# Where the second tile's state of GLA and HGRN lies: a buffer of its own, or a slot of the gates' tiles

## The chip, the cores and the metric

One core of a Trainium2 chip runs the whole program in a single launch. The metric is the device time of one execution in microseconds (us), lower is better, as the median of several runs.

## The reference, cut to what matters

Two layers of a decoder run for a prompt of 2048 tokens and for a sample of 8 rows of 8 tokens, with the same weights. Each layer projects its input once and feeds four recurrent mixers (retention, HGRN2, GLA, RWKV-7), gates their outputs, projects them back, and then attends to 256 memory tokens. GLA and HGRN are the same recurrence with different gates:

```python
def step(S, inp):                          # one chunk: q, k, v and the log gates g
    b = jnp.cumsum(gi, axis=2)
    o = einsum('bhjm,bhmv->bhjv', scores, vf) + einsum('bhjk,bhkv->bhjv', qf * exp(b), S)
    S_new = exp(b_last)[..., None] * S + einsum('bhmk,bhmv->bhkv', kf * exp(b_last - b), vf)
    return S_new, o
```

The state `S` is carried from chunk to chunk. The kernel takes chunks of 128 tokens, called tiles here.

## The kernel before, in words

**Tiling.** The prompt is cut into 4 blocks of 512 tokens (4 tiles) per layer, so there are 8 blocks. Block 0 of each layer, called a *sample block* here, also carries the 64 sample tokens. Weights stream through three-slot buffers (`wraw` for the loaded weight, `whl` for its two rounded parts; GpSimd makes the second part, line 227), and the large projections, called *dense* here, go through the two PSUM buffers `psd`.

**Order within a sample block** (`block`, then `gates`, then `finish`). Dense projections for RWKV; RWKV of the prompt in two halves (pool `wk1`), then RWKV of the sample (pool `wk1s`); dense for GLA; GLA of the prompt in two halves of two tiles each (pool `wk2`, opened anew for each half), then GLA of the sample (`wk5`); dense for HGRN (`hg_f`, `hg_q`, `hg_i`); HGRN of the prompt in two halves (`wk3`); dense for retention; retention of all four tiles (`wk4`, `R_ret`); then the gates, which need tiles `oh` of pool `wkf`. In the other blocks GLA and HGRN take all four tiles at once, and pools `wk1s` and `wk5` do not occur there.

**The order of the instructions** is made by a planner at build time. It takes program order as priority, shifted by the table `PRI`, and lets independent chains run beside each other; each engine then executes its own queue strictly in the order planned.

**GLA and HGRN of a half** (`R_gla`, `R_hgrn`): `dyadic` multiplies the gates into the queries and keys level by level and builds the scores `sT` (lines 755 and 838 to 840 in the trace); `totok` turns the keys; `outputs` makes the states `Sx` (memset at line 609, written at line 622), reads them with the queries, and normalizes. `Sx` holds the state of the half's second tile. It comes from pool `wk2` or `wk3` in sample blocks, and from the weight buffers in the others.

**The tag `th`** of the long-lived pool `dnp` has two slots of 2 KB per partition. In program order a sample block asks it for: GLA's keys `dn_gk` (line 1287), four tiles for the sigmoid of `hg_q` (`silu2`, line 523: prompt and sample for each of two column groups), eight tiles `th` of the gates (line 1282), two of the cross-attention. A tile takes whichever slot is free, and the tiles of one tag get their slots in the order in which the program asks.

**Pools on one partition.** Pools on the left side are stacked upward, pools on the right side downward from byte 229,344. By the shapes of their tiles, `wk1s` covers bytes 173,760 to 216,064 and `wk5` 173,760 to 192,576. On the right `wk2` of a sample block takes 12,032 bytes (217,312 to the top), and `wk3` takes 13,312 (216,032 to the top), of which `Sx` has 512 and 1,024. A pool may lie on bytes of one that was closed before it in program order; it then waits until that other pool's tiles there have been used for the last time. `wk4` and `wkf` lie on the bytes of `wk1s` and `wk5`.

Of the kernel before, what the change touches and what calls it, by code (L numbers as in the profile page):

```python
# [10 lines left out]
F32 = mybir.dt.float32  # L11
# [11 lines left out]
TB = 512  # L23
# [110 lines left out]
def decoder(ctx, tc, I, C, O):  # L134
# [7 lines left out]
    def pool(name, bufs=1, **kw):  # L142
        return tc.tile_pool(name=name, bufs=bufs, **kw)
# [42 lines left out]
    dnp = ctx.enter_context(pool("dnp"))  # L186
# [8 lines left out]
    def PS(kind="r"):  # L195
        kind = "d" if kind == "d" else lane[0]
        if kind == "ac":
            kind = "ac"[turn[0]]
            turn[0] ^= 1
        p = {"d": psd, "a": psa, "b": psb, "c": psc}[kind]  # L200
        return p.tile([128, 512], F32, name="ps" + kind, tag=kind)
# [17 lines left out]
    def mm(out, lhsT, rhs, start=True, stop=True):  # L219
        with held():  # L220
            PE.matmul(out, lhsT=lhsT, rhs=rhs, start=start, stop=stop, skip_group_check=True)  # L221
# [4 lines left out]
    def tt(e, out, a, b, op):  # L226
        e.tensor_tensor(out, a, b, op)  # L227
# [16 lines left out]
    for name, (o, shape) in C["layout"].items():  # L244
        n = math.prod(shape[1:])
        x = (u8 if name in U8PACK else ct)[:shape[0], o:o + n]
        if len(shape) > 2:
            ax = "abc"[:len(shape) - 1]
            x = x.rearrange(f"p ({' '.join(ax)}) -> p {' '.join(ax)}", **{k: v for k, v in zip(ax, shape[1:])})
# [35 lines left out]
    def sample_const(name, wp):  # L285
        t = wp.tile(list(C[name].shape), F32, name="s_" + name, tag="s_" + name)
        dma(t, C[name])
        return t
# [252 lines left out]
    def head_norm(o, P, nt, eps, center, wp, sqtag, evac):  # L541
        n4 = nt * NH
        o4 = o.rearrange("p t (h d) -> p (t h) d", d=64)
        st = wp.tile([128, 16], F32, name="hst", tag="hst", bufs=2)
        if center:
            V.tensor_reduce(st[:P, :n4], o4, AX.X, ALU.add)
            V.tensor_scalar(st[:P, :n4], st[:P, :n4], -1.0 / 64, None, ALU.mult)
            tt(V, o4, o4, bc(st[:P, :n4].unsqueeze(2), [P, n4, 64]), ALU.add)
        sq = wp.tile([128, n4, 64], F32, name="hsq", tag=sqtag[0], bufs=sqtag[1])
        A.activation(sq[:P, :n4], o4, AF.Square)  # L550
        ss = wp.tile([128, 16], F32, name="hss", tag="hss", bufs=2)
        V.tensor_reduce(ss[:P, :n4], sq[:P, :n4], AX.X, ALU.add)  # L552
        ri = wp.tile([128, 16], F32, name="hri", tag="hri", bufs=2)
        rsq(ri[:P, :n4], ss[:P, :n4], 1.0 / 64, eps, wp)
        tt(V, o4, o4, bc(ri[:P, :n4].unsqueeze(2), [P, n4, 64]), ALU.mult)
        ps = PS("t").rearrange("p (c n) -> p c n", c=2)
        for c in range(2):
            for t in range(nt):
                tr(ps[:, c, t * P:(t + 1) * P], o[:, t, c * 128:(c + 1) * 128], P)
        evac(ps[:, :, :nt * P])  # L560
# [23 lines left out]
    def masked_q(q, bm, wp):  # L584

        qx = wp.tile([128, SB, SN], F32, name="qx", tag="qx", bufs=2)
        tt(V, qx, bc(q.unsqueeze(1), [128, SB, SN]), bm, ALU.mult)
        return qx

    def expand(v, wp, name):  # L590

        vx = wp.tile([128, SB, 64], F32, name=name, tag=name, bufs=2)
        tt(G, vx[:SN], bc(v.unsqueeze(1), [SN, SB, 64]), bc(K["bmaskT"].unsqueeze(2), [SN, SB, 64]), ALU.mult)
        return vx[:SN].rearrange("p b d -> p (b d)")

    def outputs(seg, score, v, qd, S, NG, NC, kT, tot, wp, eps, center, evac, state_out=None):

        P, nt = seg.P, seg.nt  # L600
        KD = 128 // NG
        NP = NG // 2
        if not seg.sample:
            es = [slice(0, 64), slice(64, 128)]
            if nt > 2 and not center:
                x = wrp.tile([128, nt - 1, NC, 128], F32, name="Sx", tag="w")
            else:
                x = wp.tile([128, nt - 1, NC, 128], F32, name="Sx", tag="Sx")
            G.memset(x, 0.0)
            St = [S] + [x[:, t] for t in range(nt - 1)] + [S]  # L610
            pu = PS("r")[:, :nt * NC * 64].rearrange("p (t c n) -> p t c n", t=nt, c=NC)
            for t in range(nt):
                for h in range(NH):
                    c, g = divmod(h, NG)
                    mm(pu[g * KD:(g + 1) * KD, t, c, :], kT[:, t, h * KD:(h + 1) * KD], v[:, t, h * 64:(h + 1) * 64])

            def move(t):
                for c in range(NC):
                    for p in range(2):
                        gs = slice(64 * p, 64 * p + 64)  # L620
                        a, b = (y[gs, c, p * 64:(p + 1) * 64] for y in St[t:t + 2])
                        V.scalar_tensor_tensor(b, a, tot(t, c)[gs], pu[gs, t, c, :], ALU.mult, ALU.add)  # L622
            for t in range(nt - 1):
                move(t)
            pos = []
            for t0 in range(0, nt, 2):
                po = PS("r").rearrange("p (t n) -> p t n", t=2)
                p5 = po.rearrange("p t (c g j d) -> p t c g j d", c=NC, g=2, j=NP)
                for t in range(t0, t0 + 2):
                    for c in range(NC):  # L630
                        for j in range(NP):
                            for e in es:
                                mm(p5[e, t - t0, c, :, j, :], qd[:, c, j, t * 128 + e.start:t * 128 + e.stop], St[t][:, c, :], True, False)
                            for g in range(2):
                                h = c * NG + g * NP + j
                                x = score(t, h)
                                for e in es:
                                    mm(po[e, t - t0, h * 64:(h + 1) * 64], x[:, e], v[:, t, h * 64:(h + 1) * 64], False, True)
                pos.append(po)
            move(nt - 1)  # L640
            tags = ("rqT", "rkT", None) if center else ("qx2", "qx2", 2)
            for t0, po in zip(range(0, nt, 2), pos):
                o = wp.tile([128, 2, 256], F32, name="osb", tag=tags[0], bufs=tags[2])
                A.activation(o, po, AF.Copy)
                head_norm(o, 128, 2, eps, center, wp, tags[1:], lambda ps: evac(ps, t0 * 128))
            return
        bm = sample_const("bmask", wp)
        pa = PS("r")
        for h in range(NH):
            c, g = divmod(h, NG)  # L650
            mm(pa[:SN, h * 64:(h + 1) * 64], score(0, h), v[:SN, 0, h * 64:(h + 1) * 64])
        o = wp.tile([128, 1, 256], F32, name="osb", tag="osb")
        A.activation(o[:SN, 0], pa[:SN, :256], AF.Copy)
        pg = [PS("r") for _ in range(NG)]
        qx = [masked_q(qd[:, c, :], bm, wp) for c in range(NC)]
        for two in range(0, NH, 2):
            heads = [(j, *divmod((j * NG + two // 2) if NC == 2 else two + j, NG)) for j in range(2)]
            for b in range(SB):
                for j, c, g in heads:
                    gs = slice(g * KD, (g + 1) * KD)  # L660
                    mm(pg[g][j * SN:(j + 1) * SN, :64], qx[c][gs, b, :], S[gs, c, b, :], b == 0, b == SB - 1)
            for j, c, g in heads:
                x = o[:SN, 0, (c * NG + g) * 64:(c * NG + g + 1) * 64]
                tt(V, x, x, pg[g][j * SN:(j + 1) * SN, :64], ALU.add)
        head_norm(o[:SN, 0:1], SN, 1, eps, center, wp, ("hsq", None), evac)
        for c in range(NC):
            pu = PS("r")
            for g in range(NG):
                h = c * NG + g
                vx = expand(v[:SN, 0, h * 64:(h + 1) * 64], wp, "vx")  # L670
                mm(pu[g * KD:(g + 1) * KD, :], kT[:SN, 0, h * KD:(h + 1) * KD], vx)
            tot(c)
            tt(V, S[:, c], S[:, c], pu.rearrange("p (b d) -> p b d", b=SB), ALU.add)
        state_out()
# [1371 lines left out]
```

## Time and profile before

| | us |
|---|---|
| median of 3 runs | 3620.43 |
| lowest, highest | 3615.89, 3628.23 |
| the profiled execution | 3610.52 |
| its span, first to last instruction | 3608.7 |

The granted TensorE clock is 0.956 of full speed over the span. The trace is read by stage: the span is far longer than any wait in it, and the change touches only two stretches, the sample blocks of layer 0 (about 140 to 500 us of the span) and of layer 1 (about 1880 to 2260 us). PE stands for TensorE's matmuls, DVE for VectorE, ACT for ScalarE, POOL for GpSimd.

### The profile page before, as it was taken

What the parts mean: (1) busy time and instruction counts of PE and PEld (TensorE: products, weight loads), DVE (VectorE), ACT (ScalarE), POOL (GpSimd) and SP (SyncE); (2) the same over time, 40 slices, a digit from 0 to 9 for tenths busy, and PEclk for the clock granted to TensorE, in tenths of its full rate; (3) what the DMA queues carried; (4) which work ended last, traced back from release to release, by engine and by line L of the source; (5) the groups of instructions that cost most, each with busy time, mean ns of one, the idle gap of its engine ahead of it and who ended that gap; (6) DMA issues with size and microseconds to landing.
All of it is one profiled execution on the core that took longest, in us unless ns stands there. A gap on an engine that the chain in (4) does not pass through costs nothing.

```text
span 3608.7 us, 85093 instructions
## 1 busy us (share of the span) xinstructions
PE 3342.4 (93%) x36126; PEld 2834.0 (79%) x36126; DVE 2069.8 (57%) x5631; ACT 1254.4 (35%) x2655; POOL 538.4 (15%) x632
## 2 busy tenths in 40 slices
PE   7898899999999999999999987999979999999998
PEld 5777687777978888888877856878868788877887
DVE  5665654775436744575456456467653467446754
ACT  4442234322243324332344323443322433244323
POOL 3313230111000100011122232211100011000100
PEclk8999799999999999999999977999989999999999
DMA  6424464236552254325543352542545522543255
GB/s 191 169 88 143 119 228 173 86 90 216 194 196 98 82 193 152 124 73 198 173 172 110 119 156 99 207 145 97 146 150 205 170 98 99 192 148 115 81 201 188
DMA packets 241952, 530.74 MB, mean 147 GB/s; under 512 B 66854, under 2 KB 179750, under 8 KB 197542
## 3 DMA queue, kind: packets, MB, share of 16 engines
q1 hardware_dynamic: 241574, 525.31, 42.6%
q8 instruction: 285, 4.67, 0.5%
q14 instruction: 93, 0.76, 0.1%
HBM read 410.10 MB, written 115.16 MB: 146 GB/s over the span
## 4 chain that ended last, share of the span: by engine, by line
PE 71%; DVE 17%; ACT 5%; issue 4%; DMA 3%; POOL 2%; SPq 0%; ACTq 0%; POOLq 0%; DVEq 0%
PE psd L221 38%; PE psa L221 12%; PE psc L221 11%; PE psb L221 4%; PE psa L263 2%; PE psb L263 2%; PE psc L263 2%; DVE rsq L227 1%; DMA wraw<-in_w_in 1%; DVE Sx L622 1%; POOL whl L227 1%; DVE hss L552 1%; DVE sT L755 1%; DVE osb L227 1%; DVE wosb L227 1%
## 5 line engine op out<-in xcount | busy, mean ns | idle before, releaser
L221 PE MATMUL psd<-act,whl 128*128 128x512 f32 (+1 forms) x4032 | 1014.0, 405 | 29.1 <-DVE th L1283 11.9
L221 PEld LDWEIGHTS psd<-act,whl 128*128 128x128 f32 (+1 forms) x4032 | 751.6, 191 | 211.4 <-issue 22.2
L221 PE MATMUL psd<-whl,act 128*128 128x256 f32 x3840 | 537.7, 293 | 12.3 <-POOL whl L227 8.1
L221 PEld LDWEIGHTS psd<-whl,act 128*128 128x128 f32 x3840 | 487.3, 195 | 38.2 <-issue 16.4
L227 POOL TENSOR_TENSOR whl<-wraw,whl 128x1024 fp32r<-128x1024 f32 (+1 forms) x90 | 216.0, 2406 | 354.3 <-ACT whl L349 343.9
L271 POOL TENSOR_TENSOR ri<-ri,mhalf 128x1 f32<-128x1 f32 (+1 forms) x87 | 49.8, 573 | 1129.0 <-DVE ri L270 1116.1
L221 PE MATMUL psd<-whl,oh 128*128 128x256 f32 x1152 | 211.4, 284 | 0.0
L221 PEld LDWEIGHTS psd<-whl,oh 128*128 128x128 f32 x1152 | 177.7, 189 | 1.1 <-issue 0.3
L221 PE MATMUL psd<-whl,ol 128*128 128x256 f32 x576 | 162.7, 283 | 0.0
L349 ACT ACTIVATE whl<-wraw 128x1024 fp32r<-128x1024 f32 (+1 forms) x90 | 94.2, 1048 | 104.5 <-PE psc L221 35.5
L949 ACT ACTIVATE Xb<-X 32x256 f32<-32x256 f32 (+1 forms) x164 | 67.6, 412 | 143.1 <-DVE X L968 101.8
L221 PE MATMUL psb<-dn_hq,dn_hf 64*64 64x32 f32 (+1 forms) x3840 | 86.4, 234 | 30.9 <-DVE dn_hq L227 9.7
L221 PEld LDWEIGHTS psb<-dn_hq,dn_hf 64*64 64x64 f32 x3840 | 76.1, 149 | 46.8 <-issue 37.8
L221 PEld LDWEIGHTS psd<-whl,ol 128*128 128x128 f32 x576 | 108.6, 189 | 0.0
L227 DVE TENSOR_TENSOR x<-x,psd 128x256 f32<-128x256 f32 x72 | 30.3, 421 | 129.4 <-PE psd L221 129.4
L227 POOL TENSOR_TENSOR tot<-tot 128x8 f32<-128x8 f32 (+7 forms) x128 | 37.4, 293 | 409.1 <-DVE dn_gq L227 179.3
L426 ACT ACTIVATE xs<-xn 128x1024 f32<-128x1024 f32 (+1 forms) x34 | 35.9, 1055 | 173.4 <-PE psb L263 143.8
L755 DVE COPY_PREDICATED sT<-upack,psb 128x256 f32<-128x256 uint8 (+1 forms) x200 | 76.7, 428 | 30.6 <-PE psb L221 29.2
L1283 DVE SCALAR_TENSOR_TENSOR th<-th,psd 128x512 f32<-128x512 f32 x48 | 32.3, 686 | 95.1 <-ACT th L1282 95.0
L221 PEld LDWEIGHTS psd<-hts,wraw 128*64 128x64 f32 x1984 | 67.8, 141 | 20.3 <-issue 9.1
L221 PE MATMUL psa<-whl,oh 128*128 128x256 f32 x448 | 82.8, 283 | 0.0
L221 PE MATMUL psc<-whl,oh 128*128 128x256 f32 x448 | 82.7, 282 | 0.0
(776 smaller groups left out, 6844.7 us busy)
## 6 DMA issues: line engine op xcount, KB each, us to landing
whl<-w_w_out SPq DMA_DIRECT2D x56, 1024.0 KB
wraw<-in_w_in SPq DMA_DIRECT2D x76, 512.0 KB
wraw<-in_w_out SPq DMA_DIRECT2D x32, 512.0 KB
w_w_out<-whl SPq DMA_DIRECT2D x16, 1024.0 KB
x<-x SPq DMA_DIRECT2D x32, 512.0 KB
whl<-w_rw_r SPq DMA_DIRECT2D x12, 1024.0 KB
whl<-w_rw_k SPq DMA_DIRECT2D x12, 1024.0 KB
whl<-w_rw_v SPq DMA_DIRECT2D x12, 1024.0 KB
```

The source lines that it names most:

```text
L221: PE.matmul(out, lhsT=lhsT, rhs=rhs, start=start, stop=stop, skip_group_check=True)
L227: e.tensor_tensor(out, a, b, op)
L263: PE.transpose(out, in_, ident[:rows, :rows])
L271: G.tensor_tensor(y, y, mhalf[:P], ALU.pow)
L349: A.activation(hl[:, 0], raw, AF.Copy)
L426: A.activation(out, xt, AF.Square, accum_out=ss[:P])
L552: V.tensor_reduce(ss[:P, :n4], sq[:P, :n4], AX.X, ALU.add)
L622: V.scalar_tensor_tensor(b, a, tot(t, c)[gs], pu[gs, t, c, :], ALU.mult, ALU.add)
L755: V.copy_predicated(out, bc(mk, [P, w, 32 // s, s]), ps)
L949: A.activation(dst(b), src(b), AF.Copy)
L1283: V.scalar_tensor_tensor(th, th, 1.0, x, ALU.add, ALU.mult)
```

## The change

In `outputs`, for GLA and HGRN in blocks where a part has two tiles, `Sx` is no longer allocated from the part's pool; it is the first 128 or 256 columns of a tile of tag `th` in `dnp`. Retention (`center`) keeps the pool's buffer, and the four-tile blocks keep the weight buffers. `wk2` becomes 512 bytes smaller in sample blocks and `wk3` 1,024 bytes smaller. No instruction is added or removed.

```diff
             if nt > 2 and not center:
                 x = wrp.tile([128, nt - 1, NC, 128], F32, name="Sx", tag="w")
+            elif center:
+                x = wp.tile([128, nt - 1, NC, 128], F32, name="Sx", tag="Sx")
             else:
-                x = wp.tile([128, nt - 1, NC, 128], F32, name="Sx", tag="Sx")
+                x = dnp.tile([128, TB], F32, name="Sx", tag="th", bufs=2)[:, :NC * 128].rearrange("p (t c n) -> p t c n", t=1, c=NC)
             G.memset(x, 0.0)
```

## Rows read from the trace of the kernel before

**Rows 1.** The page's busy time: engine, us, share, instructions; PEld is weight loads.

```profile
PE 3342.4 (93%) x36126; PEld 2834.0 (79%) x36126; DVE 2069.8 (57%) x5631; ACT 1254.4 (35%) x2655; POOL 538.4 (15%) x632
```

**Rows 2.** Busy time by stretch: stretch, us, busy (count) per engine, PE clock, DMA.

```profile
260.00:280.00 20.00, 19.24 (x338) 17.06 (x336) 8.41 (x31) 6.89 (x14) 0.00 (x0) 1.00 0.18 54
...
440.00:460.00 20.00, 11.75 (x238) 10.29 (x240) 15.15 (x57) 3.90 (x10) 2.23 (x7) 0.50 0.01 2
...
2200.00:2220.00 20.00, 11.17 (x216) 9.64 (x216) 15.47 (x56) 6.17 (x14) 1.96 (x7) 0.58 0.01 2
```

**Rows 3.** By tile: HGRN's last input and first step, layer 0 block 0.

```profile
L524 DVE SCALAR_TENSOR_TENSOR dn_hq<-th,psd x2: 679/684/689, 229.5 to 243.1; 128x512 f32<-128x512 f32 x2
...
L838 DVE TENSOR_SCALAR ha<-dn_hf,c,c x4: 395/411/1127, 369.5 to 433.0; 128x256 f32<-128x256 f32 x4
```

**Rows 4.** The same for layer 1 block 0, then layer 0 block 2.

```profile
L524 DVE SCALAR_TENSOR_TENSOR dn_hq<-th,psd x2: 677/682/687, 1961.3 to 1974.9; 128x512 f32<-128x512 f32 x2
...
L838 DVE TENSOR_SCALAR ha<-dn_hf,c,c x4: 398/404/413, 2134.7 to 2190.4; 128x256 f32<-128x256 f32 x4
...
L524 DVE SCALAR_TENSOR_TENSOR dn_hq<-th,psd x2: 674/678/681, 1156.6 to 1168.8; 128x512 f32<-128x512 f32 x2
...
L838 DVE TENSOR_SCALAR ha<-dn_hf,c,c x2: 540/816/1093, 1173.0 to 1181.8; 128x512 f32<-128x512 f32 x2
```

**Rows 5.** Order of time: the end of sample RWKV, then HGRN, in both layers.

```profile
358.26 0.46 POOL L227 TENSOR_TENSOR ons_rwkv<-ons_rwkv,og 128x128 f32<-128x128 f32 x1 [0.31 <-ACT og L1273]
358.66 0.32 POOL L609 MEMSET Sx<- 128x256 f32 x1
...
2134.14 0.42 DVE L227 TENSOR_TENSOR wosb<-wosb,hri 64x256 f32<-64x256 f32 x1
...
2134.68 0.72 DVE L838 TENSOR_SCALAR ha<-dn_hf,c,c 128x256 f32<-128x256 f32 x2
```

**Rows 6.** By tile: retention's first transposes and the gates' first rounding, three blocks.

```profile
L263 PE MATMUL psc<-fpack,dn_rq x8: 272/273/330, 403.0 to 403.9; 128*128 128x128 f32 x8
...
L1486 ACT ACTIVATE oh<-th x8: 614/631/634, 461.7 to 491.4; 128x512 fp32r<-128x512 f32 x8
...
L263 PE MATMUL psc<-fpack,dn_rq x8: 421/421/473, 2164.3 to 2165.8; 128*128 128x128 f32 x8
...
L1486 ACT ACTIVATE oh<-th x8: 612/626/634, 2218.7 to 2250.0; 128x512 fp32r<-128x512 f32 x8
...
L263 PE MATMUL psc<-fpack,dn_rq x8: 272/272/273, 838.1 to 838.9; 128*128 128x128 f32 x8
...
L1486 ACT ACTIVATE oh<-th x8: 617/627/636, 874.4 to 914.8; 128x512 fp32r<-128x512 f32 x8
```

**Rows 7.** HGRN's matmuls in block 1 of layer 0: busy by stretch, two tiles.

```profile
715.00:800.00 85.00, 12.75 (x512) 9.99 (x512) 6.72 (x9) 0.92 0.31 92
...
715.00:800.00 85.00, 4.36 (x96) 3.97 (x96) 1.19 (x2) 0.92 0.31 92
```

**Rows 8.** Order of time: last read of `dn_gk`. By tile: retention's last input.

```profile
252.57 0.38 PE L263 MATMUL psb<-fpack,dn_gk 128*128 128x128 f32 x2
...
L1287 ACT ACTIVATE dn_rv<-psd x2: 597/597/597, 341.4 to 355.7; 128x512 f32<-128x512 f32 x2
```

**Rows 9.** Dense work alone (tile `psd`) in the stretch after `hg_q`'s first sigmoid.

```profile
234.00:254.00 20.00, 13.35 (x103) 10.95 (x103) 1.11 (x3) 1.02 (x3) 1.00 0.38 132
```

**Rows 10.** Order of time: one GLA multiply alone, one beside a GpSimd split.

```profile
235.23 0.38 DVE L227 TENSOR_TENSOR dn_gq<-dn_gq,tot 128x256 f32<-128x256 f32 x1
...
238.83 2.39 POOL L227 TENSOR_TENSOR whl<-wraw,whl 128x1024 fp32r<-128x1024 f32 x1 [2.83 <-ACT whl L349]
...
239.50 2.00 DVE L227 TENSOR_TENSOR dn_gq<-dn_gq,tot 128x256 f32<-128x256 f32 x1
```

**Rows 11.** The gates' first tiles, and half of a dense group of 24 matmuls.

```profile
L1282 ACT ACTIVATE th<-gs x2: 631/632/632, 367.2 to 379.0; 128x512 f32<-128x512 f32 x2
...
405.16 3.02 PE L221 MATMUL psd<-act,whl 128*128 128x512 f32 x12
```

## The prediction, made before the changed kernel was run

> **What bounds the kernel now.** The page first: TensorE has matmuls running for 3342 of 3609 us [rows 1], so time can only come from stretches in which it waits or runs at the lower clock. The table of busy time by stretch shows where these lie: in the middle of a sample block TensorE is busy for 19.24 of 20 us at full clock, but before the gates for 11.75 of 20 us at granted clock 0.50, and in layer 1 for 11.17 at 0.58 [rows 2]. 0.50 is the 1.2 GHz level; before it the engine had only the small matmuls of two recurrences, since the dense work had run out. What runs there? The view by tile answers: HGRN. In layer 0 its last input is ready at 243 us, its first step starts at 369.5 us [rows 3]. In layer 1 it waits from 1975 to 2134.7 us; in an ordinary block from 1168.8 only to 1173.0 us [rows 4].
>
> What does it wait for? The order of time shows that HGRN's memset follows sample RWKV's last GpSimd instruction within 0.4 us, and that in layer 1 `ha` starts 0.5 us after sample RWKV's last use of `hri` [rows 5]. These are bytes: `wk1s` ends at 216,064 and `wk3` begins at 216,032, so 32 bytes of `ha` lie on the last buffer of `hri`. HGRN does not wait for sample GLA (`wk5`), which ends far lower: `ha` starts at 369.5 us, retention, which does lie on `wk5`'s bytes, at 403.0 us [rows 3, 6]. So the wait goes by overlap, not by program order.
>
> **The change part by part.** *Pool `wk3`* loses 1,024 bytes and then begins at 217,056, above `wk1s`. The wait is gone, and HGRN can start when GLA's second half and `hg_q` are done, at about 262 us in layer 0 and 1990 us in layer 1 (estimates: 9 us after `dn_gk`'s last read at 252.6 us [rows 8], since `hg_q` must follow it, see below). It then runs beside the rest of prompt RWKV and beside sample RWKV. `wk2` loses 512 bytes; it overlapped no left pool before, so nothing follows.
>
> What is late next? The chain of the left pools: sample RWKV, sample GLA, retention, then `oh`, each lying on the one before. HGRN's start does not shorten the first two by anything I can read, so I take nothing there. Retention is shortened. Its stage, from first transposes to the first rounding of a gate, takes 461.7 - 403.0 = 58.7 us in layer 0 and 2218.7 - 2164.3 = 54.4 us in layer 1, with HGRN's second half in the same VectorE and TensorE queues; in block 1 of layer 0, where HGRN is over by then, it takes 874.4 - 838.1 = 36.3 us [rows 6]. Gains: 22.4 and 18.1 us, 40.5 us in all.
>
> *The cost of HGRN's new place.* Its matmuls are 12.75 + 4.36 = 17.1 us of TensorE in a block where they run at nearly full clock [rows 7], and they now stand in a stretch where TensorE has 0.8 us in 20 free [rows 2]. All of it would be lost if each matmul pushed the chain of the left pools; nothing, if it pushed only dense work, which has time: retention's last input is ready at 355.7 us and retention starts at 403.0 us, 47 us later [rows 6, 8]. A block therefore pays 0 to 17.1 us. I take 5, near the lower end, because the planner ranks RWKV before HGRN and the dense work has that cover; 10 us for both blocks.
>
> *The two slots of `th`.* Now GLA's `Sx` tiles stand in the line for them. The first gets the free slot after `dn_gk`, long before it is needed. The second takes the slot that the first gives back. Then both slots are held, by `dn_gk` and by `Sx`, and the first sigmoid of `hg_q`, whose product stands at 229.5 us today, must wait for `dn_gk`'s last read at 252.6 us [rows 3, 8]. Behind it the two `psd` buffers fill, and all dense work stops. In that stretch it took 13.35 us of TensorE [rows 9]. What hides this: GLA and RWKV go on alone and faster, and the dense work comes later. With HGRN's share retention's last input moves from 355.7 to about 355.7 + 13.4 + 17.1 = 386 us, still ahead of 403.0 us. I cost it at nothing; if that cover is gone it costs 13.35 us per block. The chain that waits for `dn_gk`'s release, GLA itself, is not held up by anything of the dense work, so no circle forms.
>
> HGRN's two `Sx` tiles take both slots next and give them back at the end of each half, before which no gate can be evaluated. RWKV's two gate tiles used the slots at 367.2 and 379.0 us [rows 11]. HGRN's first half takes 433.0 - 369.5 = 63.5 us today [rows 3]; two such halves from 262 us on end by 389 us (an estimate). The gate tiles may then come up to 22 us late, which is hidden, since `oh` waits for retention's end in any case. Nothing is lost. The memsets stay on GpSimd; HGRN's takes 0.32 us [rows 5], and behind a waiting one stand the weight splits of 2.4 us [rows 10], which the dense work waits for. That wait exists today as well, for a buffer of the pool.
>
> A rule speaks against the new place. A GLA multiply takes 0.38 us alone and 2.00 us when it starts during a GpSimd split [rows 10]. The Trainium skill, "SBUF — State Buffer", section "Who interferes with whom", says that VectorE instructions with two SBUF inputs and GpSimd instructions that read SBUF exclude each other for a whole instruction; these rows agree. HGRN would meet more splits in the dense stage; each costs it 1.6 us, on a chain that is then off the end.
>
> **Sum.** 40.5 - 10 = 30.5 us. The profiled execution took 3610.5 us, 9.9 us below the median, and would take 3580; on the median, 3620.4 - 30.5 = 3590 us. Bounds: with no contention, and with sample GLA in layer 0 (358.7 to 403.0 us, 44 us) as short as in layer 1 (2134.6 to 2164.3 us, 30 us [rows 5, 6]), 40.5 + 14 = 55 us, and some 5 us more if HGRN fills idle TensorE instead of pushing anything: 3560. With the full 17.1 us in each block, 40.5 - 34.2 = 6 us: 3614.
>
> **The rivals.** *No gain, because the slots turn into the new wait.* The dense stop of 13.35 us per block comes back as time: 3620.4 - 30.5 + 26.7 = 3617 us. For it: all dense work goes through two `psd` buffers and one sigmoid blocks them. Against it: the 47 us of cover. It decides when retention's last input is later than the end of sample GLA. The Trainium skill, "Perfetto Trace Analysis", section "Optimization Strategy", says that a gap repeating on the engine that should be saturated can mean that there is not enough SBUF for the next tile; by it, more users of two slots means such gaps.
>
> *Slower: HGRN stays late and holds the slots.* If the 32 bytes are not what HGRN waits for, the change doesn't do what it is read to do. Then HGRN's `Sx` tiles hold both slots from about 262 us until its halves end at about 433.0 us [rows 3] and 461.7 us [rows 6], RWKV's gate tiles at 367.2 and 379.0 us [rows 11] must wait, and the two dense groups of GLA's gates, which lie ready in `psd` today, are made only after that: 2 groups of 2 x 3.02 us [rows 11] in each of two blocks, 24 us: 3645 us. It decides as soon as HGRN's first half ends after 367.2 us. For it: only two blocks show the overlap. Against it: the 0.5 us in layer 1 and the ordinary block.
>
> **How the numbers follow.** The forecast of 3590 us (3560 to 3614) has 0.70, the slots as the new wait 0.18, HGRN late 0.12. The predicted time is 3590 us. The range has to reach the second case, 3617 us, with the measurement's 0.2% above it: 3560 to 3625; it leaves out the third case and some of the ends. A measurement can tell 0.3%, about 11 us, from no change. Faster by more than that 0.70, within it 0.18, slower 0.12.
>
> **What would show it.** Right: `ha` starts near 262 and 1990 us; TensorE is no longer at 0.50 with HGRN's matmuls before the gates; retention's stage falls to about 36 us; `hg_q`'s sigmoids start at about the last read of `dn_gk`; retention's last input is ready before its first transposes. Wrong: `ha` still follows the last `hri` of sample RWKV; RWKV's gate tiles come after HGRN's end; or sample RWKV is longer by more than retention is shorter.

## The result and the profile after

| | before | after |
|---|---|---|
| median | 3618.16 us (4 runs) | 3567.20 us (4 runs) |
| ratio, with its 95% interval | | 0.9868 (0.9848 to 0.9889) |
| the profiled execution, its span | 3610.52, 3608.7 | 3566.24, 3564.4 |
| granted clock over the span | 0.956 | 0.968 |

By the ratio the changed kernel is faster by 1.3%: 48 us, between 40 and 55; the two medians are 51 us apart. The prediction had 3590 us, a gain of 30.5 us, with a range from 3560 to 3625 us. The sign was right, and the overlap as a cause; the size was not, and what made up the difference was not in the sum.

The view by tile of the changed kernel, layer 0 block 0, answers to [rows 3, 6, 8] (line numbers have moved by two):

```profile
L524 DVE SCALAR_TENSOR_TENSOR dn_hq<-th,psd x2: 687/687/687, 251.2 to 260.6; 128x512 f32<-128x512 f32 x2
L840 DVE TENSOR_SCALAR ha<-dn_hf,c,c x4: 410/410/415, 261.8 to 323.3; 128x256 f32<-128x256 f32 x4
L263 PE MATMUL psc<-fpack,dn_rq x8: 421/421/478, 397.3 to 398.9; 128*128 128x128 f32 x8
L1289 ACT ACTIVATE dn_rv<-psd x2: 598/598/599, 404.0 to 409.7; 128x512 f32<-128x512 f32 x2
L1488 ACT ACTIVATE oh<-th x8: 613/633/635, 440.2 to 478.0; 128x512 fp32r<-128x512 f32 x8
```

HGRN's first step stands at 261.8 us, where it stood at 369.5 [rows 3]; the sigmoids of `hg_q` now come after GLA's last use of `dn_gk`. The same for layer 1 block 0, with the copy of `dn_gk` that begins GLA there:

```profile
L1289 ACT ACTIVATE dn_gk<-psd x1: 597/597/597, 1866.1 to 1866.1; 128x512 f32<-128x512 f32 x1
L840 DVE TENSOR_SCALAR ha<-dn_hf,c,c x4: 406/408/410, 1978.9 to 2035.9; 128x256 f32<-128x256 f32 x4
L263 PE MATMUL psc<-fpack,dn_rq x8: 272/273/328, 2138.3 to 2139.2; 128*128 128x128 f32 x8
L1488 ACT ACTIVATE oh<-th x8: 613/631/634, 2171.5 to 2206.6; 128x512 fp32r<-128x512 f32 x8
```

In the kernel before, that copy of `dn_gk` starts here:

```profile
L1287 ACT ACTIVATE dn_gk<-psd x1: 597/597/597, 1883.1 to 1883.1; 128x512 f32<-128x512 f32 x1
```

It splits the 44.3 us between the two spans (3608.7 - 3564.4): 1883.1 - 1866.1 = 17.0 us were gained before it, most of it in layer 0's sample block, and 27.3 us behind it, nearly all of it in layer 1's sample block. By stage, with [rows 6]:

| | layer 0 | layer 1 |
|---|---|---|
| retention starts sooner | 403.0 - 397.3 = 5.7 | 26.0 - 17.0 = 9.0 |
| its stage is shorter | 58.7 - 42.9 = 15.8 | 54.4 - 33.2 = 21.2 |
| gates, first to last rounding, are longer | 29.7 - 37.8 = -8.1 | 31.3 - 35.1 = -3.8 |
| the rest | 3.6 | 0.9 |
| sum | 17.0 | 27.3 |

The busy time by stretch answers to [rows 2] (columns as there); two more stretches are added.

```profile
260.00:280.00 20.00, 19.59 (x440) 17.24 (x438) 14.11 (x42) 7.94 (x17) 4.34 (x7) 1.00 0.23 81
420.00:440.00 20.00, 19.92 (x131) 16.71 (x132) 17.41 (x40) 7.88 (x12) 6.14 (x3) 1.00 0.92 277
440.00:460.00 20.00, 15.72 (x67) 12.61 (x66) 15.55 (x26) 8.28 (x13) 6.05 (x3) 0.91 0.75 270
2160.00:2180.00 20.00, 3.97 (x18) 2.80 (x15) 13.73 (x41) 6.93 (x12) 0.00 (x0) 0.58 0.22 70
2200.00:2220.00 20.00, 19.99 (x154) 19.06 (x153) 11.45 (x17) 6.25 (x11) 9.65 (x4) 1.00 0.84 281
```

The reader is to see two new limits. In layer 0 TensorE is now full before the gates (19.92 of 20 us, at full clock), 17.35 us of it dense work. In layer 1 it has run out of work instead: 3.97 of 20 us at clock 0.58, while retention's last normalizations run mainly on VectorE (13.73 us).

And the dense work in the stretch of [rows 9], where it had 13.35 us:

```profile
234.00:254.00 20.00, 1.66 (x35) 0.66 0.23 81
```

The dense stop that the prediction described is real: 1.66 us of dense work are left there, and the clock fell to 0.66. Nevertheless the kernel is faster than the sum said.

### The profile page after: what moved, and what is told of

Its sections match the earlier page's. It is cut to its first block, busy times and chain, and to the rows that moved or that the text cites. A ratio compares the mean times of both kernels' runs of the same rounds, so it can differ in the third digit from the quotient of the medians.

```text
span 3564.4 us, 85069 instructions
## 1 busy us (share of the span) xinstructions
PE 3314.5 (93%) x36126; PEld 2814.3 (79%) x36126; DVE 2075.4 (58%) x5631; ACT 1253.4 (35%) x2655; POOL 535.9 (15%) x632
## 4 chain that ended last, share of the span: by engine, by line
PE 70%; DVE 18%; ACT 4%; DMA 3%; issue 3%; POOL 2%; SPq 0%; ACTq 0%; POOLq 0%; DVEq 0%
PE psd L221 38%; PE psa L221 11%; PE psc L221 11%; PE psb L221 4%; PE psa L263 2%; PE psb L263 2%; PE psc L263 2%; DVE rsq L227 1%; DVE Sx L624 1%; DMA wraw<-in_w_in 1%; DVE osb L227 1%; DVE hss L552 1%; POOL whl L227 1%; DVE hri L283 1%; DVE sT L757 1%
## 5 line engine op out<-in xcount | busy, mean ns | idle before, releaser
L227 POOL TENSOR_TENSOR tot<-tot 128x16 f32<-128x16 f32 (+7 forms) x128 | 36.4, 284 | 399.3 <-DVE dn_gq L227 182.8
L221 PE MATMUL psb<-dn_hq,dn_hf 64*64 64x32 f32 (+1 forms) x3840 | 78.6, 222 | 6.2 <-DVE dn_hq L227 3.8
L221 PEld LDWEIGHTS psb<-dn_hq,dn_hf 64*64 64x64 f32 x3840 | 68.6, 136 | 19.9 <-issue 11.5
L221 PE MATMUL psd<-hts,wraw 128*64 128x64 f32 x1984 | 79.0, 231 | 3.9 <-DVE th L1285 3.8
```

## The experiments

Four questions: does the overlap by bytes hold HGRN? What does its removal bring alone? What do the slots do, and whose? By what?

### The overlap taken away, without the slots

The kernel before, with the spare buffer of `hri` gone where it has the sample's 64 rows, so that `wk1s` ends at 216,000:

```diff
-        ri = wp.tile([128, 16], F32, name="hri", tag="hri", bufs=2)
+        ri = wp.tile([128, 16], F32, name="hri", tag="hri", bufs=1 if P < 128 else 2)
```

> The kernel before, with one buffer instead of two for `hri` where it has 64 rows (the sample). `Sx` stays in its own buffer; `wk1s` ends at 216,000, below `wk3`'s 216,032. Overlap alone (the slots cost and bring nothing): `ha` of layer 0 starts at about 250 us, since `hg_q` needs no wait for a slot, and the time is that of the changed kernel, 3567 us within 11. Slots as cost: the dense stop behind `dn_gk` is gone, up to 2 x 13 us better than the changed kernel, 3541 us. Slots as help: the gates' tiles come early again and their dense groups stand in front of sample RWKV, which in layer 1 stays some 50 us long instead of 39; 3585 to 3600 us. Something else than the overlap holds HGRN: `ha` at 369 us and 3618 us.

Measured: 3593.05 us, ratio 0.9938 (0.9920 to 0.9956). HGRN's places, by tile, layer 0:

```profile
L524 DVE SCALAR_TENSOR_TENSOR dn_hq<-th,psd x2: 681/684/687, 227.3 to 240.7; 128x512 f32<-128x512 f32 x2
L838 DVE TENSOR_SCALAR ha<-dn_hf,c,c x4: 401/411/1057, 263.5 to 330.5; 128x256 f32<-128x256 f32 x4
```

The overlap did hold HGRN, and freeing it brings 22 us (16 to 29). That is less than the forecast of 30.5 and about half of what the change gains. Of the expectations, slots as help fits in its time, between 3585 and 3600 us, and in sample RWKV of layer 1, which takes even 56.3 us. The reason given for it does not fit: RWKV's gate tiles do not come early (421.8 us in layer 0, 431.6 in the changed kernel, 367.2 before). `ha` came at 263.5 us and not at 250, no sooner than in the changed kernel, though `hg_q` was ready 20 us earlier.

### The same from the other side: 64 bytes

The changed kernel with an unused buffer in `wk3` where HGRN has two tiles, of 1,024 bytes as here or of 960 (`[128, 240]`):

```diff
+                if NC == 2:
+                    wp.tile([128, 256], F32, name="pad", tag="pad")
```

> The changed kernel, with an unused buffer of 1,024 bytes in `wk3` where HGRN has two tiles, so that `wk3` begins at 216,032 as before and overlaps `wk1s`; both `Sx` in the slots. If the overlap holds HGRN: `ha` after the last `hri` of sample RWKV (about 360 us in layer 0), and the slots are held late: the third case of the prediction, 3645 us; at least 3618. If what frees HGRN is that `Sx` left its pool: `ha` at 262 us and 3567 us.

> The changed kernel, with an unused buffer of 960 bytes in `wk3`, 64 bytes less than in the padded kernel that took 3629 us: `wk3` begins at 216,096, above `wk1s`' end at 216,064. If the overlap by bytes decides: `ha` at 262 us and 3567 us. If the size of the pool or its use of memory as such matters: between 3567 and 3629 us.

Measured: 3629.07 us with 1,024 bytes, ratio 1.0034 (1.0021 to 1.0047), and 3568.66 us with 960 bytes, ratio 0.9892 (0.9874 to 0.9910). Layer 0 with 1,024 bytes (line numbers have moved by four):

```profile
L842 DVE TENSOR_SCALAR ha<-dn_hf,c,c x4: 399/400/402, 353.2 to 431.2; 128x256 f32<-128x256 f32 x4
L1286 ACT ACTIVATE th<-gs x2: 629/630/630, 417.1 to 466.0; 128x512 f32<-128x512 f32 x2
```

and with 960 bytes:

```profile
L842 DVE TENSOR_SCALAR ha<-dn_hf,c,c x4: 406/410/415, 257.1 to 317.6; 128x256 f32<-128x256 f32 x4
```

64 bytes of a buffer that nothing reads or writes are worth over 50 us: the ratios differ by 0.0142, 51 us, and the medians by 60 us, of which 4.5 us is the difference between the kernel before in the two rounds of runs (3616.04 and 3611.53 us). The 1,024-byte kernel is the prediction's second rival made real: HGRN late, the gates' tiles (367.2 and 379.0 us in [rows 11]) behind it at 417.1 and 466.0. It is slower than the kernel before by 12 us (8 to 17); the prediction had priced it at 24.

### Whose slots

GLA's `Sx` (`NC == 1`) back in its own pool, HGRN's in the slots; then the other way round (`NC == 2`), with the spare `hri` buffer gone as above, so that `wk3` keeps clear of `wk1s`:

```diff
-            elif center:
+            elif center or NC == 1:
                 x = wp.tile([128, nt - 1, NC, 128], F32, name="Sx", tag="Sx")
```

> The changed kernel, with GLA's `Sx` back in a buffer of pool `wk2`; HGRN's `Sx` stays in a slot of `th`, `wk3` stays above `wk1s`. If GLA's part of the slots costs the dense stop: `hg_q`'s sigmoids at 229 us again and up to 26 us better than the changed kernel, 3541 us. If GLA's slots cost nothing: 3567 us. If the slots of GLA bring something by holding dense work back from RWKV: as the kernel with own buffers and no overlap, above 3580 us.

> The changed kernel, with HGRN's `Sx` back in a buffer of pool `wk3`, GLA's `Sx` in the slots, and one buffer of `hri` for the sample, so that `wk3` at 216,032 lies above `wk1s` (216,000). If HGRN's use of the slots costs or brings nothing: 3567 us within 11. If HGRN's slots, held until its halves end, hold the gates' tiles back (367 us before, 432 us in the changed kernel) and this costs time: RWKV's gate tiles come at about 370 us and the time is 10 to 20 us lower. If this holding back is what shortened sample RWKV: 15 us higher.

Without overlap in any of the four, the medians are:

| | HGRN's `Sx` in its own buffer | in a slot |
|---|---|---|
| GLA's `Sx` in its own buffer | 3593.05 | 3599.13, ratio 0.9953 (0.9939 to 0.9968) |
| in a slot | 3572.03, ratio 0.9884 (0.9864 to 0.9904) | 3567.20 |

HGRN's slots bring and cost nothing that stands out in both rows (+6 and -5 us). GLA's bring 21 to 32 us, so the third expectation of the first kernel (above 3580 us) and the first of the second (3567 within 11) held. The prediction had costed both at nothing, and only feared a loss.

### The wait of `hg_q` taken away, the slots kept

GLA's slots do one thing to others: the sigmoids of `hg_q` have to wait for `dn_gk`'s last read. In this kernel they take the buffer of tag `gs`, in sample blocks only; both `Sx` stay in the slots. In a second kernel, which has `bool(smp) and l == 0` for `bool(smp)`, this is so in layer 0 alone.

```diff
-    def silu2(ps, out, n, wp):
-        th = wp.tile([128, TB], F32, name="th", tag="th", bufs=2)
+    def silu2(ps, out, n, wp, gs=False):
+        th = wp.tile([128, TB], F32, name="th", **(dict(tag="gs") if gs else dict(tag="th", bufs=2)))
...
-                proj_c("hg_q", i * 128, lambda ps: silu2(ps, hq[:, i, :], TB, gp), lambda ps: silu2(ps, hqs[:, i, :], SN, gp))
+                proj_c("hg_q", i * 128, lambda ps: silu2(ps, hq[:, i, :], TB, gp, bool(smp)), lambda ps: silu2(ps, hqs[:, i, :], SN, gp, bool(smp)))
```

> The changed kernel, but in sample blocks the sigmoids of `hg_q` take the buffer of tag `gs` instead of a slot of `th`. Both `Sx` stay in the slots; only the wait of `hg_q` for `dn_gk`'s last read is gone, and with it the dense stop. If that wait is what shortens sample RWKV in layer 1 (by leaving dense work to stand beside it): `hg_q`'s first sigmoid at about 228 us, sample RWKV of layer 1 some 56 us long at a granted clock near 0.8, and the time of the kernel with own buffers and no overlap, 3593 us within 11. If the wait costs time, as the prediction's second case has it: below 3567 us, down to 3541. If the gain comes from something else in the slots: 3567 us.

> As the run before, but only in layer 0; in layer 1 `hg_q` still waits for `dn_gk` in the line for the slots. If the wait brings its gain in layer 1 alone and costs some 3 us in layer 0 (19.7 against 17.0 us gained there): layer 1's sample RWKV is 41 us long at a clock near 1.0 and the time is 3564 us, between 3556 and 3572. If the gain hangs on layer 0's order too: above 3580 us.

> The changed kernel unchanged, on the chip of these runs, as what the three others are compared with: 3567 us within 6.

Measured: 3595.57 us, ratio 0.9956 (0.9943 to 0.9969), without the wait; 3574.24 us, ratio 0.9899 (0.9882 to 0.9916), without it in layer 0 alone; 3565.50 us, ratio 0.9878 (0.9861 to 0.9894), for the changed kernel again. The wait is the cause: taking it away in both layers gives back 30 us, as the first expectation has it, though every `Sx` lies where it lay. Most of it is layer 1's: 21 us lie between the two kernels that differ there alone (3595.57 and 3574.24). Without the wait in layer 0 alone the loss is 9 us, and the time is 2 us above the range that was expected, though layer 1's sample RWKV is as forecast (41.8 us at clock 1.00). The intervals of that kernel and the changed one overlap, and the profiles of the kernels without the wait in layer 0 reach layer 1's `dn_gk` from 2.7 us sooner to 12.6 us later than the changed kernel; so whether the wait gains in layer 0 stays open.

Where does layer 1 lose it? The largest part in sample RWKV. Busy time and clock from its first `vx` to its last GpSimd instruction, first without the wait, in this kernel:

```profile
2073.30:2129.50 56.20, 49.40 (x493) 36.68 (x494) 31.42 (x82) 18.12 (x42) 21.06 (x18) 0.79 0.43 132
```

in the kernel with own buffers and no overlap:

```profile
2060.30:2116.60 56.30, 49.49 (x493) 36.78 (x493) 31.39 (x82) 18.19 (x42) 21.01 (x18) 0.79 0.44 135
```

in the changed kernel:

```profile
2061.10:2102.60 41.50, 38.72 (x536) 29.80 (x529) 31.02 (x95) 15.36 (x39) 17.70 (x19) 1.00 0.42 131
```

and in the kernel before, where HGRN is not yet there:

```profile
2083.20:2136.00 52.80, 47.23 (x326) 29.93 (x326) 28.78 (x64) 16.19 (x33) 24.88 (x16) 0.79 0.60 193
```

With the wait the stretch takes 41.5 us at clock 1.00 (41.4 to 41.8 us in the five profiles with it in layer 1 and no overlap); without it 56.2 to 57.2 us at 0.73 to 0.79 (three profiles). TensorE's work is nearly the same: 49.40 x 0.79 = 39.0 us at full clock, an estimate, against 38.72. So of the 14.7 us, about 49.40 - 38.72 = 10.7 us is the lower clock.

Is it that more dense work stands beside sample RWKV? The same two stretches for dense work alone (TensorE's busy time with its count, clock, DMA), without the wait and in the changed kernel:

```profile
2073.30:2129.50 56.20, 21.35 (x163) 0.79 0.43 132
2061.10:2102.60 41.50, 17.08 (x166) 1.00 0.42 131
```

It is not: there are 163 and 166 dense matmuls, and 21.35 x 0.79 = 16.9 us of work against 17.08. What the wait holds back comes later still. Layer 1 by stage, in us, with the granted clock and the count of dense matmuls:

| | without the wait | changed kernel |
|---|---|---|
| from the copy of `dn_gk` to sample RWKV | 197.5, 0.96, 909 | 195.0, 0.96, 808 |
| sample RWKV | 56.2, 0.79, 163 | 41.5, 1.00, 166 |
| from there to retention's first transposes (sample GLA) | 43.2, 0.83, 83 | 35.7, 0.90, 156 |
| retention's stage | 27.9, 0.62, 0 | 33.2, 0.78, 24 |
| gates, first to last rounding | 34.9, 0.83, 115 | 35.1, 0.82, 115 |
| sum | 359.7 | 340.5 |

The 101 dense matmuls that are held back stand beside sample GLA (73 more) and in retention's stage (24 more); sample GLA is shorter with them, retention's stage longer. Both kernels with GLA's `Sx` in its own buffer have the counts of the left column, within one. The profiled executions of the table are 36.4 us apart: 19.2 here, 9.7 before and 7.5 behind it.

How the clock falls can be read in the order of time of the kernel with own buffers and no overlap, layer 1:

```profile
2057.27 1.70 PE L221 MATMUL psd<-whl,act 128*128 128x256 f32 x12
2057.80 0.42 DVE L227 TENSOR_TENSOR dn_hf<-dn_hf,tot 128x256 f32<-128x256 f32 x1
...
2062.56 3.43 DVE L227 TENSOR_TENSOR qx<-ar,s_bmask 128x512 f32<-128x512 f32 x2
...
2062.83 5.39 POOL L227 TENSOR_TENSOR whl<-wraw,whl 128x1024 fp32r<-128x1024 f32 x2
...
2066.31 2.19 DVE L227 TENSOR_TENSOR dn_hf<-dn_hf,tot 128x256 f32<-128x256 f32 x1
...
2070.48 0.70 PE L221 MATMUL psb<-dn_hq,dn_hf 64*64 64x64 f32 x16 [3.41 <-DVE dn_hq L227]
...
2071.69 2.93 PE L221 MATMUL psd<-whl,act 128*128 128x256 f32 x12
...
2087.54 1.15 PE L221 MATMUL psa<-Ss,qx 64*64 64x64 f32 x32
...
2092.24 1.14 PE L221 MATMUL psc<-Ss,qx 64*64 64x64 f32 x30 [1.34 <-DVE qx L227]
...
2097.00 1.10 PE L221 MATMUL psa<-Ss,qx 64*64 64x64 f32 x15
```

There are two falls. First two weight splits on GpSimd hold VectorE (a multiply of 0.42 us takes 2.19), TensorE stands idle for 3.41 us at the head of one of HGRN's steps, and right behind it 12 dense matmuls take 2.93 us where 12 took 1.70 before: the lower level. The clock is 0.50 from 2072 to 2076 us and back at 1.00 from 2080 to 2092 us. The second fall costs more. It comes 2 us after an idle time of 1.34 us, in which TensorE waits for VectorE's `qx`: the clock is 0.50 from 2094 to 2110 us, where 15 matmuls take what 32 of the same form took before. For 12 us of this stretch no dense work stands there. But the same steps of the changed kernel have none either (2089 to 2097 us), and run at 1.00. So it is not shown what keeps the clock up there; the profiles show the order of the work and the idle times to differ, and no run separates the two.

The rule of the Trainium skill that the prediction cited ("SBUF — State Buffer", "Who interferes with whom") agrees here again: 2.19 us against 0.42, 1.8 us more, where the prediction took 1.6. The idle time of TensorE came on top; how much of it is the block's was not separated.

That clock and time go together is shown by one program: the executions of the kernel without the wait run the same instructions in the same order, and take from 3582.46 us at clock 0.966 over the span to 3602.62 us at 0.959. A line through the eleven of them falls by 2.3 us per 0.001; which of the two moves the other it does not say. The median clock of these eleven is 0.960, that of the changed kernel's eight executions 0.967; 0.007 by this line is 16 us, about half of the 30 us between the two kernels. The other half was not separated either.

## Why the prediction was right and wrong

**The overlap: right.** HGRN waited for 32 bytes. `ha` was forecast for 262 us and came at 261.8; 1990 us in layer 1 was 1978.9. Two points are inexact. By the kernel's text the bytes belong to a second buffer of `hri` that the sample part, with a single `head_norm`, never uses, so that the wait goes by reserved bytes. And HGRN's last input is not `hg_q` but its values `dn_hv`, copied from 254.4 to 270.5 us in layer 0 and from 1989.4 to 2001.6 in layer 1; the wait was shorter by that, but real.

**The sum, term by term.** With the overlap alone taken away, its two terms can be read by themselves. Layer 0 of that kernel, then layer 1:

```profile
L1287 ACT ACTIVATE dn_gk<-psd x1: 597/597/597, 142.2 to 142.2; 128x512 f32<-128x512 f32 x1
L263 PE MATMUL psc<-fpack,dn_rq x8: 271/272/327, 391.7 to 393.9; 128*128 128x128 f32 x8
L1486 ACT ACTIVATE oh<-th x8: 614/632/635, 436.4 to 473.5; 128x512 fp32r<-128x512 f32 x8
...
L1287 ACT ACTIVATE dn_gk<-psd x1: 597/597/597, 1863.4 to 1863.4; 128x512 f32<-128x512 f32 x1
L263 PE MATMUL psc<-fpack,dn_rq x8: 421/421/478, 2159.6 to 2161.2; 128*128 128x128 f32 x8
L1486 ACT ACTIVATE oh<-th x8: 612/632/633, 2187.6 to 2222.6; 128x512 fp32r<-128x512 f32 x8
```

In layer 0 the copy of `dn_gk` starts at 143.0 us before and at 144.4 in the changed kernel. What each stretch gains in the profiled executions, in us, layer 0 + layer 1:

| | forecast | overlap alone | the change |
|---|---|---|---|
| retention's stage | 40.5 | 14.0 + 26.4 = 40.4 | 15.8 + 21.2 = 37.0 |
| from `dn_gk` to retention's first transposes | -10 | 10.5 - 15.0 = -4.5 | 7.1 + 9.0 = 16.1 |
| gates, first to last rounding | 0 | -7.4 - 3.7 = -11.1 | -8.1 - 3.8 = -11.9 |
| the rest | 0 | -3.9 | 3.1 |
| sum | 30.5 | 20.9 | 44.3 |

**Retention's stage: right.** Forecast were about 36 us in both layers. The changed kernel has 42.9 in layer 0, where dense work now fills TensorE (19.92 of 20 us), and 33.2 in layer 1. One of the prediction's own signs of being right, retention's last input ready ahead of its first transposes, failed in layer 0: 409.7 against 397.3 us, where it had estimated 386 against 403.

**The gates' stretch: a term put at nothing.** The prediction ended its sum at the first rounding of a gate. From there to the last rounding both kernels take 11 to 12 us longer than the kernel before; this, and not HGRN's new place, is the larger part of why the overlap alone brought less than 30.5 us. What makes it longer was not looked for.

**HGRN's new place, 5 us per block: wrong in each block, and near in the sum by luck.** It was bounded from 0 to 17.1 us and taken near the lower end on the ground that dense work, which has time, would give way. In layer 0 the stretch became 10.5 us shorter, in layer 1 it became 15.0 us longer. The dense work did give way, but it meets the chain of the left pools later. In layer 1 the 15.0 us lie almost wholly between the end of sample RWKV and retention, where sample GLA runs: 43.0 us with 83 dense matmuls (21.0 us busy), against 28.3 us with none before. Sample RWKV itself took 52.8 us before and 56.3 then, both at clock 0.79. In layer 0 sample GLA's stretch lost 50 of its 133 dense matmuls and became 7.7 us shorter. That the dense work makes sample GLA longer was not tested by itself.

**The slots at nothing, with 13.35 us of loss as the other end: the sign was missed.** The stop happened as described and where described. The prediction asked what hides it, found the cover, and stopped there. It did not ask what the delayed queue does to the clock of the stretches behind. In layer 1 sample RWKV ran at 0.79 and now runs at 1.00, with no more dense work beside it than without the wait; GLA's slots are worth 21 to 32 us, as much as the overlap or more. The bound "below nothing too" was not drawn for this term, though the prediction's own sentence (GLA and RWKV go on alone and faster) and the clock of 0.50 in [rows 2] were at hand. That the number came as near as it did is luck: two errors of opposite sign, 8 us too much for the overlap, 21 to 32 us too little for the slots.

**The rivals.** The slots as the new wait did not happen; the rule of the Trainium skill cited for it ("Perfetto Trace Analysis", "Optimization Strategy") lets one take a gap like that of 234 to 254 us for a shortage of memory. It is one here, but the kernel without it is 30 us slower. HGRN late with the slots held exists, and is slower, but only with the overlap put back; its price was 12 us and not 24.

**What else was forecast.** In layer 0 TensorE no longer runs at 0.50 with HGRN's matmuls alone before the gates (1.00 at 420 to 440 us); in layer 1 HGRN's matmuls are gone from there, but the clock is still 0.58 at 2160 to 2180 us. `hg_q`'s sigmoids come at `dn_gk`'s last read: 247.9 after 247.2 us. RWKV's gate tiles come later, but for another reason than the one given, and by more than the 22 us: 431.6 and 435.5 us in layer 0, and 431.8 and 435.8 with HGRN's `Sx` in its own buffer, where it holds no slot. They come after HGRN's end, which the prediction had named a sign of being wrong (its last output is copied at 391.1 us in layer 0 and 2085.5 in layer 1, the gate tiles come from 431.6 and 2116.1); the overlap was the cause all the same, so this sign did not tell the cases apart.

## What to carry to other kernels

Count the reserved bytes on which two pools meet, spare buffers too: 64 bytes decided over 50 us here, and a smaller spare buffer removes such a wait as well as a moved tile does. Work that has cover isn't priced when it is delayed until it is clear what TensorE does in the stretches behind, where the same queue also serves the chain that ends last: the delay was worth 30 us here, with the same amount of work. And before a gain is put down to more work standing somewhere, count what stands there in both kernels; here the count was the same, and the clock was not.

## What the runs showed of the hardware

In the kernel with own buffers and no overlap TensorE was idle for 3.41 us after work at full clock; the matmuls behind it ran at granted clock 0.50 (2072 to 2076 us), and those from 2080 us on at 1.00 again. 2 us after an idle time of only 1.34 us the clock fell again, and stayed at 0.50 from 2094 to 2110 us though the engine was busy for all of these 16 us. In one and the same program the granted clock over the span varied from 0.959 to 0.966 between executions, and the time by 20 us with it. The eight executions of the changed kernel lie between 0.967 and 0.971 and between 3562 and 3575 us.
